# A streaming-encoder step on one core: low sums over four PSUM banks, a root multiplied on GpSimd, activations a step sooner

## The chip, the cores and the metric

The kernel runs on one core of a Trainium2 chip. A core has five engines with queues of their own: TensorE (PE; its weight loads are listed as PEld), VectorE (DVE), ScalarE (ACT), GpSimd (POOL) and SyncE (SP), which here only issues DMAs. The metric is the device time of one execution in microseconds (us).

## The reference, cut to what matters

One layer of an encoder is computed for two request groups that share the weights: 256 frames of a new stream and 64 of a running one. The kernel treats them as T = 320 columns beside each other. All data is float32 with D = 2048 features. The part around the change is the feed-forward half, with D_FF = 5632:

```python
hn = rmsnorm(h, norm_ffn[l])
gu = hn @ w_gate_up[l]
h = h + (jax.nn.silu(gu[..., :D_FF]) * gu[..., D_FF:]) @ w_down[l]
```

Ahead of it come one combined input projection, stick-breaking attention, a spatial gate, two branch projections and an output projection; behind it a last norm.

## The kernel before, in words

Features lie on the 128 partitions, so a weight block is 128 x 128. A float32 product is made of pieces of reduced type: ACT casts a raw weight tile to `wh` (the high part), DVE subtracts to get `wl` (the low part), and activations are split in the same way into a pair. A product then is weight-high times activation-high, plus weight-high times activation-low, plus weight-low times activation-high.

The feed-forward products run in **quads** (`quad`, L542): four output blocks of 128 features at once, 30 quads in all. 22 of them make gates and ups, alternating (a gate quad, then the up quad that belongs to it), 8 of them a part of the down product. A quad has two stages.

- **The main sums** (L565) turn the product round: the activations are the weights of TensorE, and the `wh` of four blocks stream through, 512 columns wide. For each pair of the 16 k-blocks a raw tile of 512 KB is loaded by SP (L549), ACT casts it (L557), DVE subtracts (L558), and ten matmuls follow. 80 matmuls fill three PSUM banks, `main`. Quads alternate between the `acc` banks (three) and the `aux` banks (four).
- **The low sums** (L575): for each of the four blocks b, 16 matmuls of 320 columns with the `wl` as weights, into one bank, which DVE then copies to `total` (L576). The banks were `aux1` (there is one), `aux`, `aux1`, `aux`. So the third block wants the bank that the first has filled, and its first matmul waits until DVE has copied it.

The main sums come out with frames on the partitions and have to be transposed. `quad_turn` takes the upper and the lower 16 bits of each word apart: ACT copies the first plane out of the three banks (L592), DVE the second (L594), and ACT issues one transposing DMA for each (L595). `quad_join` puts the planes together again (L605) and adds them to `total` (L607, L608).

A table of due ticks (`at`, `tick`) sets when this happens; a tick is one weight tile or one low block. Joining is due 10 ticks behind the end of the main sums (6 for the last up quad), so in the middle of the next quad. One and two ticks later the two halves of `total` go on. For a gate (`gate_out`): times `rh`, the reciprocal root of the norm, on DVE (L612), then SiLU on ACT (L613). For an up (`up_out`): times `rh` (L617), times the gate (L618), both on DVE, then a cast on ACT (L621) and subtractions on DVE (L624) that split the result into the pair `act`. So in the quad behind an up quad DVE has more to do than in the quad behind a gate quad.

Buffers near by: three raw tiles, four `wh`, four `wl` and five more low tiles (`low`), two `sum` tiles. Instructions of one engine run in the order in which they stand in its queue.

Of the kernel before, what the change touches and what calls it, by code (L numbers as in the profile page):

```python
# [11 lines left out]
U16 = mybir.dt.uint16  # L12
AF = mybir.ActivationFunctionType
ALU = mybir.AluOpType

P = 128
TP = 256
TS = 64
T = TP + TS
# [15 lines left out]
def stream_step(ctx: ExitStack, tc: tile.TileContext, xT, w_in, w_a, w_b, w_out, w_gu, w_down,  # L35
                gains, ws_t, bs, ck_t, cv, y_t, k_t, v_t, sv_t):
    nc = tc.nc
# [11 lines left out]
    def aux():  # L49
        return psum.tile([P, 512], F32, tag="aux", bufs=4, name="aux")  # L50

    def aux1():
        return psum.tile([P, 512], F32, tag="aux1", bufs=1, name="aux1")
# [4 lines left out]
    def at(tick, fn, *a):  # L58
        assert tick > state["tick"], (tick, state["tick"])
        later.setdefault(tick, []).append((fn, a))  # L60

    def tick():
        state["tick"] += 1
        for fn, a in later.pop(state["tick"], ()):
            fn(*a)

    def halved(raw, n):
        wh = wsplit.tile([P, HALF * P], F32R, tag="wh", name="wh")
        wl = wsplit.tile([P, HALF * P], F32R, tag="wl", name="wl")
        nc.scalar.copy(out=wh[:, : n * P], in_=raw[:, : n * P])  # L70
        state["split"] = nc.vector.tensor_tensor(out=wl[:, : n * P], in0=raw[:, : n * P],  # L71
                                                 in1=wh[:, : n * P].bitcast(F32), op=ALU.subtract)
        return wh, wl

    def weights(src, n):
        state["n"] += 1
        if state["more"] is not None and state["n"] > 3 and state["n"] % 2 == 0:
            raw = state["more"].tile([P, HALF * P], F32, tag="raw2", bufs=3, name="raw2")
        else:
            raw = wraw.tile([P, HALF * P], F32, tag="raw", name="raw")  # L80
        nc.sync.dma_start(out=raw[:, : n * P], in_=src)
        return halved(raw, n)
# [8 lines left out]
    def block(src, act):  # L91
        ps = acc()
        nk = len(act)
        for k0 in range(0, nk, HALF):
            n = min(HALF, nk - k0)
            w = weights(src[:, k0 * P : (k0 + n) * P], n)
            for j in range(n):
                product(ps, w, j, act[k0 + j], k0 + j == 0, k0 + j == nk - 1)
            tick()
        return ps[:, :T]  # L100

    def pair(name, shape=(2, T), dt=F32):
        return big.tile([P, *shape], dt, tag="D", bufs=24, name=name)
# [10 lines left out]
    def t320(tag, bufs=2, dt=F32):  # L114
        return tmp.tile([P, T], dt, tag=tag, bufs=bufs, name=tag)
# [43 lines left out]
    got = {}  # L159
# [36 lines left out]
    with tc.manual_schedule(engines={mybir.EngineType.SP}):  # L196
        load_x(0, 0, 1)
        for i, (b0, nb, c, n) in enumerate(tiles):
# [11 lines left out]
            w = halved(raw, nb * n)  # L210
# [220 lines left out]
    for g in range(H):  # L431
        ps = block(w_in[4 * H + g], xs)
        t = t320("ev")
# [51 lines left out]
    for g in range(H):  # L485
        ps = block(w_in[3 * H + g], xs)
        t = t320("ev")
# [5 lines left out]
    for m in range(KD):  # L493
        gate = []
        for i in range(2):
            ps = block(w_in[5 * H + i * KD + m], xs)
            t = t320("ev")
# [8 lines left out]
        ps = block(w_a[m], aT)  # L506
        t = t320("sq", 1)
        nc.vector.tensor_tensor(out=t, in0=ps, in1=gate[0], op=ALU.mult)
        ps = block(w_b[m], bT)
# [10 lines left out]
    for m in range(KD):  # L520
# [4 lines left out]
        ps = block(w_out[m], merged)  # L525
# [14 lines left out]
    count = [0, 0]  # L540

    def quad(src, xs, done, tag="sum", lag=10):  # L542
        lows = []
        nk = len(xs)
        main = [(acc, aux)[count[1] % 2]() for _ in range(3)]
        count[1] += 1
        for c in range(0, nk, 2):
            raw = wraw.tile([P, HALF * P], F32, tag="raw", name="raw")
            nc.sync.dma_start(out=raw.rearrange("p (b k) -> p b k", b=4),  # L549
                              in_=src[:, :, c * P : (c + 2) * P].rearrange("b p k -> p b k"))  # L550
            wh = wsplit.tile([P, HALF * P], F32R, tag="wh", name="wh")
            if count[0] % 9 < 4:
                wl = wsplit.tile([P, HALF * P], F32R, tag="wl", name="wl")
            else:
                wl = fpool.tile([P, HALF * P], F32R, tag="low", bufs=5, name="low")
            count[0] += 1
            nc.scalar.copy(out=wh, in_=raw)  # L557
            state["split"] = nc.vector.tensor_tensor(out=wl, in0=raw, in1=wh.bitcast(F32), op=ALU.subtract)  # L558
            wh = wh.rearrange("p (b k) -> p b k", b=4)
            lows.append(wl)  # L560
            for j in range(2):
                k = c + j
                w, x = wh[:, :, j * P : (j + 1) * P], xs[k]
                for i, at0 in enumerate((0, T + TS, P, T + TS + P, TP)):
                    nc.tensor.matmul(main[i // 2].rearrange("p (b m) -> p b m", b=4), x[:, at0 : at0 + P], w,  # L565
                                     start=k == 0 and i % 2 == 0, stop=k == nk - 1 and (i % 2 == 1 or i == 4))
            tick()
        total = fpool.tile([P, 4, T], F32, tag=tag, bufs=2 if tag == "sum" else 1, name=tag)
        now = state["tick"]
        turning = quad_turn(main)  # L570
        for b in range(4):
            ps = aux1() if b % 2 == 0 else aux()
            for k in range(nk):
                at0 = (2 * b + k % 2) * P
                nc.tensor.matmul(ps[:, :T], lows[k // 2][:, at0 : at0 + P], xs[k][:, 0:T], start=k == 0, stop=k == nk - 1)  # L575
            copied = nc.vector.tensor_copy(total[:, b, :], ps[:, :T])  # L576
            tick()
        at(now + lag, quad_join, copied.ins, total, *turning)
        for i in range(2):
            at(now + lag + 1 + i, done, total, 2 * i)  # L580
        return total

    def quad_turn(main):
        flat = fpool.tile([P, 12 * P], F32, tag="flat", name="flat")
        turned = fpool.tile([P, 2, 12, P], U16, tag="turned", name="turned")
        planes = flat.bitcast(U16).rearrange("p (i n) -> p i n", i=2)
        for i in range(2):
            for c in range(3):
                hw = main[c].bitcast(U16).rearrange("p (n w) -> p n w", w=2)
                plane = planes[:, i, c * 512 : (c + 1) * 512]  # L590
                if i == 0:
                    tc.keep_in_program_order(nc.scalar.copy(out=plane, in_=hw[:, :, 1 - i]))  # L592
                else:
                    nc.vector.tensor_copy(plane, hw[:, :, 1 - i])  # L594
            nc.scalar.dma_start_transpose(out=turned[:, i], in_=planes[:, i, :])  # L595
        return flat, turned

    def quad_join(behind, total, flat, turned):
        with tc.issue_after(behind), tc.issue_after(state["split"].ins):
            join(total, flat, turned)  # L600
# [9 lines left out]
    def gate_out(total, b):  # L610
        t = total[:, b : b + 2, :]
        nc.vector.tensor_tensor(out=t, in0=t, in1=got["rh"][:, None, :].to_broadcast([P, 2, T]), op=ALU.mult)  # L612
        nc.scalar.activation(out=t, in_=t, func=AF.Silu)  # L613

    def up_out(to, apart, gate, total, b):
        t = total[:, b : b + 2, :]
        nc.vector.tensor_tensor(out=t, in0=t, in1=got["rh"][:, None, :].to_broadcast([P, 2, T]), op=ALU.mult)  # L617
        nc.vector.tensor_tensor(out=t, in0=t, in1=gate[:, b : b + 2, :], op=ALU.mult)  # L618
        for j in range(2):
            a = pair("act", dt=F32R)  # L620
            nc.scalar.copy(out=a[:, 0, :], in_=t[:, j, :])  # L621
            flat = a.rearrange("p i t -> p (i t)")
            for r0, r1, at0 in (((TP, T, T), (0, TP, T + TS)) if apart else ((0, T, T),)):
                nc.vector.tensor_tensor(out=flat[:, at0 : at0 + r1 - r0], in0=t[:, j, r0:r1],  # L624
                                        in1=a[:, 0, r0:r1].bitcast(F32), op=ALU.subtract)
            to.append(a)
# [72 lines left out]
    def gate_quad(b0, tag="sum"):  # L699
        return quad(w_gu[b0 : b0 + 4], wide_x, gate_out, tag)  # L700

    def up_quad(b0, gate, to, apart, lag=10):
        quad(w_gu[KF + b0 : KF + b0 + 4], wide_x, lambda total, b: up_out(to, apart, gate, total, b), lag=lag)
# [15 lines left out]
    for k0, k1 in ((0, HALF), (HALF, n)):  # L719
        for m, ps in enumerate(lead):  # L720
            w = weights(w_down[m][:, (s0 + k0) * P : (s0 + k1) * P], k1 - k0)
# [155 lines left out]
```

## Time and profile before

| what | us |
|---|---|
| median of 3 runs (lowest, highest) | 1694.61 (1692.58, 5915.3) |
| the profiled execution's own time | 1693.54 |
| span of its profile, first to last instruction | 1691.8 |
| TensorE busy in it | 1676.3 |
| VectorE busy | 1063.0 |
| ScalarE busy | 711.8 |
| GpSimd busy | 38.9 |

The highest of the three runs lies far off the other two and is not used. The profile shows one execution. Busy time of matmuls overlaps and says little of how fast they follow each other; that is read from the starts of equal groups of matmuls in the chain of waits or in the timeline, which list each group with its start, its duration and its count. "Idle before" is the time in which an engine waited just ahead of an instruction, with the engine or DMA that released it. ACTq and SPq rows are issues of DMAs.

### The profile page before, as it was taken

The page shows a single profiled execution, that of the slowest core. Times are in us where ns is not written, and L with a number is a line of the kernel's source. Part 1 is how long each engine was busy: PE and PEld are TensorE (multiplying, and loading weights), DVE is VectorE, ACT ScalarE, POOL GpSimd, SP SyncE. Part 2 cuts the span into 40 slices and gives each one's busy share as a digit, 9 for nine tenths or more (in the row PEclk, how much of TensorE's full clock was granted, in tenths as well). Part 3 has the DMA queues.
Part 4 walks back from the last instruction along what each step waited for, and adds up shares of the span by engine and source line. Part 5 has one row for each costly group of instructions (what it writes and reads, how often), then busy time and mean ns, then how long its engine had stood idle before and what let it go on. Part 6 is the DMA issues. An engine that isn't in the chain of part 4 may idle for free.

```text
span 1691.8 us, 25018 instructions
## 1 busy us (share of the span) xinstructions
PE 1676.3 (99%) x10112; PEld 1576.2 (93%) x10112; DVE 1063.0 (63%) x1431; ACT 711.8 (42%) x914; POOL 38.9 (2%) x68
## 2 busy tenths in 40 slices
PE   9999999999999999999999999999999999999998
PEld 9999999999999999998888888988888888888997
DVE  7665656544444445556666766566767666667766
ACT  7555655433333333444443334333434343334343
POOL 1100001000000000000000000000000000000000
PEclk9999999999999999999999999999999999999999
DMA  8766555444444444556566666666666666666554
GB/s 291 245 175 177 160 160 166 116 150 150 150 150 150 151 149 171 173 169 180 162 197 163 188 168 196 172 195 164 192 174 182 175 180 187 179 175 177 166 150 125
DMA packets 286644, 291.75 MB, mean 172 GB/s; under 512 B 123168, under 2 KB 252192, under 8 KB 286528
## 3 DMA queue, kind: packets, MB, share of 16 engines
q1 hardware_dynamic: 188592, 257.72, 47.8%
q10 hardware_dynamic: 95312, 24.17, 8.1%
q0 software_dynamic: 2624, 8.26, 1.5%
q8 instruction: 79, 1.29, 0.3%
q14 instruction: 37, 0.30, 0.1%
HBM read 256.03 MB, written 5.51 MB: 155 GB/s over the span
## 4 chain that ended last, share of the span: by engine, by line
PE 87%; DVE 6%; DMA 5%; issue 2%; ACT 0%; SPq 0%; DVEq 0%; ACTq 0%
PE aux L565 16%; PE acc L87 15%; PE acc L88 15%; PE acc L89 15%; PE aux L575 13%; PE acc L565 8%; DMA raw<-w_gu 4%; DVE low L558 1%; DVE flat L605 1%; DVE act L624 1%; PE aux L89 1%; PE aux L87 1%; PE aux L88 1%; DVE flat L594 1%; PE acc L657 1%
## 5 line engine op out<-in xcount | busy, mean ns | idle before, releaser
L557 ACT CAST wh<-raw 128x1024 fp32r<-128x1024 f32 x240 | 252.7, 1053 | 503.1 <-DMA raw<-w_gu 322.5
L70 ACT CAST wh<-raw 128x1024 fp32r<-128x1024 f32 (+2 forms) x232 | 235.7, 1016 | 412.2 <-PE acc L88 286.4
L71 DVE TENSOR_TENSOR wl<-raw,wh 128x1024 fp32r<-128x1024 f32 (+2 forms) x232 | 274.8, 1187 | 165.6 <-ACT wh L70 165.0
L87 PE MATMUL acc<-A,wh 128*128 128x320 f32 x1088 | 337.8, 311 | 0.2 <-ACT A L108 0.2
L88 PE MATMUL acc<-A,wh 128*128 128x320 f32 x1088 | 336.6, 309 | 0.0
L89 PE MATMUL acc<-A,wl 128*128 128x320 f32 x1088 | 336.3, 309 | 0.0
L87 PEld LDWEIGHTS acc<-A,wh 128*128 128x128 f32 x1088 | 204.5, 188 | 2.2 <-issue 1.5
L88 PEld LDWEIGHTS acc<-A,wh 128*128 128x128 f32 x1088 | 204.6, 188 | 0.2 <-DVE A L110 0.2
L89 PEld LDWEIGHTS acc<-A,wl 128*128 128x128 f32 x1088 | 204.4, 188 | 0.0
L565 PE MATMUL aux<-wh,A 128*128 128x512 f32 x880 | 201.6, 389 | 0.0
L565 PE MATMUL acc<-wh,A 128*128 128x512 f32 x880 | 201.5, 389 | 0.0
L558 DVE TENSOR_TENSOR low<-raw,wh 128x1024 fp32r<-128x1024 f32 x132 | 161.1, 1228 | 58.8 <-ACT wh L557 58.8
L565 PEld LDWEIGHTS aux<-wh,A 128*128 128x128 f32 x880 | 164.7, 188 | 33.7
L565 PEld LDWEIGHTS acc<-wh,A 128*128 128x128 f32 x880 | 164.8, 188 | 33.7
L558 DVE TENSOR_TENSOR wl<-raw,wh 128x1024 fp32r<-128x1024 f32 x108 | 130.9, 1220 | 50.9 <-ACT wh L557 50.9
L575 PE MATMUL aux<-A,low 128*128 128x320 f32 x784 | 131.1, 309 | 2.9 <-DVE sum L576 2.9
L575 PEld LDWEIGHTS aux<-A,low 128*128 128x128 f32 x784 | 119.2, 188 | 4.8 <-DVE sum L576 3.7
L575 PE MATMUL aux<-A,wl 128*128 128x320 f32 x624 | 107.4, 310 | 3.5 <-DVE sum L576 2.8
L576 DVE COPY sum<-aux 128x320 f32<-128x320 f32 x112 | 53.9, 487 | 84.3 <-PE aux L575 84.1
L575 PEld LDWEIGHTS aux<-A,wl 128*128 128x128 f32 x624 | 95.6, 188 | 5.6 <-DVE sum L576 3.9
L87 PE MATMUL acc<-mh,wh 128*128 128x320 f32 x256 | 79.1, 309 | 0.0
L88 PE MATMUL acc<-ml,wh 128*128 128x320 f32 x256 | 79.1, 309 | 0.0
(238 smaller groups left out, 2236.9 us busy)
## 6 DMA issues: line engine op xcount, KB each, us to landing
raw<-w_gu SPq DMA_DIRECT2D x176, 512.0 KB, 4.0
raw<-w_in SPq DMA_DIRECT2D x141, 512.0 KB, 3.7
raw<-w_down SPq DMA_DIRECT2D x80, 512.0 KB, 4.4
raw<-w_out SPq DMA_DIRECT2D x32, 512.0 KB, 3.6
raw<-w_a SPq DMA_DIRECT2D x16, 512.0 KB, 3.5
raw<-w_b SPq DMA_DIRECT2D x16, 512.0 KB, 3.5
raw<-w_down SPq DMA_DIRECT2D x16, 256.0 KB, 2.9
ev<-xT POOLq DMA_DIRECT2D x16, 160.0 KB, 2.6
```

Of the source, the lines that this page charges most:

```text
L70: nc.scalar.copy(out=wh[:, : n * P], in_=raw[:, : n * P])
L71: state["split"] = nc.vector.tensor_tensor(out=wl[:, : n * P], in0=raw[:, : n * P], in1=wh[:, : n * P].bitcast(F32), op=ALU.subtract)
L87: nc.tensor.matmul(ps[:, :T], a, x[0], start=first, stop=False)
L88: nc.tensor.matmul(ps[:, :T], a, x[1], start=False, stop=False)
L89: nc.tensor.matmul(ps[:, :T], b, x[0], start=False, stop=last)
L557: nc.scalar.copy(out=wh, in_=raw)
L558: state["split"] = nc.vector.tensor_tensor(out=wl, in0=raw, in1=wh.bitcast(F32), op=ALU.subtract)
L565: nc.tensor.matmul(main[i // 2].rearrange("p (b m) -> p b m", b=4), x[:, at0 : at0 + P], w, start=k == 0 and i % 2 == 0, stop=k == nk - 1 ...
L575: nc.tensor.matmul(ps[:, :T], lows[k // 2][:, at0 : at0 + P], xs[k][:, 0:T], start=k == 0, stop=k == nk - 1)
L576: copied = nc.vector.tensor_copy(total[:, b, :], ps[:, :T])
L594: nc.vector.tensor_copy(plane, hw[:, :, 1 - i])
L605: nc.vector.tensor_copy(rows[:, :, :, :, 1 - i], turned[:, i].rearrange("p (c b) t -> p b c t", c=3))
```

## The change

Four things change. The first two low blocks of a quad go to two of the banks of the set that this quad's main sums don't use (`others`), the third to `aux1`, the fourth to `aux`. `quad_turn` becomes two functions: `first_plane` stands where `quad_turn` stood, `second_plane` (the three DVE copies and their transposing DMA) is issued behind DVE's copy of the second low block. A gate is multiplied by `rh` once more, after SiLU, by GpSimd, and `up_out` no longer multiplies by `rh`. Both halves of a quad are due one tick behind the joining, where the second half was due two ticks behind.

```diff
     def quad(src, xs, done, tag="sum", lag=10):
         lows = []
         nk = len(xs)
-        main = [(acc, aux)[count[1] % 2]() for _ in range(3)]
+        banks, others = (acc, aux) if count[1] % 2 == 0 else (aux, acc)
+        main = [banks() for _ in range(3)]
         count[1] += 1
...
-        turning = quad_turn(main)
+        turning = first_plane(main)
         for b in range(4):
-            ps = aux1() if b % 2 == 0 else aux()
+            ps = (others, others, aux1, aux)[b]()
             for k in range(nk):
                 at0 = (2 * b + k % 2) * P
                 nc.tensor.matmul(ps[:, :T], lows[k // 2][:, at0 : at0 + P], xs[k][:, 0:T], start=k == 0, stop=k == nk - 1)
             copied = nc.vector.tensor_copy(total[:, b, :], ps[:, :T])
+            if b == 1:
+                with tc.issue_after(copied.ins):
+                    second_plane(main, *turning)
             tick()
         at(now + lag, quad_join, copied.ins, total, *turning)
         for i in range(2):
-            at(now + lag + 1 + i, done, total, 2 * i)
+            at(now + lag + 1, done, total, 2 * i)
         return total
...
+    def half_words(main, c, i):
+        return main[c].bitcast(U16).rearrange("p (n w) -> p n w", w=2)[:, :, 1 - i]
+
+    def first_plane(main):
         flat = fpool.tile([P, 12 * P], F32, tag="flat", name="flat")
         turned = fpool.tile([P, 2, 12, P], U16, tag="turned", name="turned")
+        plane = flat.bitcast(U16)[:, 0 : 12 * P]
+        for c in range(3):
+            tc.keep_in_program_order(nc.scalar.copy(out=plane[:, c * 512 : (c + 1) * 512], in_=half_words(main, c, 0)))
+        nc.scalar.dma_start_transpose(out=turned[:, 0], in_=plane)
         return flat, turned
+
+    def second_plane(main, flat, turned):
+        plane = flat.bitcast(U16)[:, 12 * P : 24 * P]
+        for c in range(3):
+            nc.vector.tensor_copy(plane[:, c * 512 : (c + 1) * 512], half_words(main, c, 1))
+        nc.scalar.dma_start_transpose(out=turned[:, 1], in_=plane)
...
     def gate_out(total, b):
         t = total[:, b : b + 2, :]
         nc.vector.tensor_tensor(out=t, in0=t, in1=got["rh"][:, None, :].to_broadcast([P, 2, T]), op=ALU.mult)
         nc.scalar.activation(out=t, in_=t, func=AF.Silu)
+        nc.gpsimd.tensor_tensor(out=t, in0=t, in1=got["rh"][:, None, :].to_broadcast([P, 2, T]), op=ALU.mult)
 
     def up_out(to, apart, gate, total, b):
         t = total[:, b : b + 2, :]
-        nc.vector.tensor_tensor(out=t, in0=t, in1=got["rh"][:, None, :].to_broadcast([P, 2, T]), op=ALU.mult)
         nc.vector.tensor_tensor(out=t, in0=t, in1=gate[:, b : b + 2, :], op=ALU.mult)
```

The lines move with it: before and after correspond as L557 and L558 (cast), L558 and L559 (subtraction), L575 and L576 (low matmuls), L576 and L577 (their copies), L592 and L595 (first plane), L594 and L602 (second plane), L595 and L596 with L603 (transposes), L605 and L612 (joining), L612 and L619, L618 and L625, L621 and L628 (cast of `act`), L624 and L631. GpSimd's multiplication is L621 of the changed kernel.

Three places show how the instructions stand. The first is TensorE in the sixth quad, an up quad whose main sums lie in `aux`: the low matmuls, of which the numbered names are tiles of `aux1`. Before:

```order
L575 MATMUL aux_8973<-A,low 128x320 x10
L575 MATMUL aux_8973<-A,wl 128x320 x6
L575 MATMUL aux<-A,low 128x320 x10
L575 MATMUL aux<-A,wl 128x320 x6
L575 MATMUL aux_9009<-A,low 128x320 x10
L575 MATMUL aux_9009<-A,wl 128x320 x6
```

and after:

```order
L576 MATMUL acc<-A,low 128x320 x10
L576 MATMUL acc<-A,wl 128x320 x6
L576 MATMUL acc<-A,low 128x320 x10
L576 MATMUL acc<-A,wl 128x320 x6
L576 MATMUL aux_9011<-A,low 128x320 x10
L576 MATMUL aux_9011<-A,wl 128x320 x6
```

The first two blocks now go to the idle `acc` banks, and only the third to `aux1`.

The second place is VectorE in the quad behind an up quad (the 27th, main sums in `acc`), where the activations are made and the low sums copied. Before:

```order
L617 TENSOR_TENSOR sum<-sum,rh 128x640 x2
L618 TENSOR_TENSOR sum<-sum,held 128x640 x2
L624 TENSOR_TENSOR act<-sum,act 128x320 x4
L594 COPY flat<-acc 128x512 x3
L576 COPY sum<-aux_13727 128x320
L576 COPY sum<-aux 128x320
L576 COPY sum<-aux_13763 128x320
L558 TENSOR_TENSOR wl<-raw,wh 128x1024 x2
```

and after:

```order
L625 TENSOR_TENSOR sum<-sum,held 128x640 x2
L631 TENSOR_TENSOR act<-sum,act 128x320 x4
L577 COPY sum<-aux 128x320 x2
L602 COPY flat<-acc 128x512 x3
L577 COPY sum<-aux_13763 128x320
L559 TENSOR_TENSOR wl<-raw,wh 128x1024 x2
```

The two multiplications by `rh` are gone, and the copies of the first two low blocks stand ahead of the second plane's copies; the two subtractions keep their place behind the third block's copy.

The third place is ScalarE in the same quad. Before:

```order
L557 CAST wh<-raw 128x1024 x7
L621 CAST act<-sum 128x320 x4
L592 COPY flat<-acc 128x512 x3
L557 CAST wh<-raw 128x1024
L595 DMA_TRANSPOSE turned<-flat 128x12x128 x2
L557 CAST wh<-raw 128x1024 x6
```

and after:

```order
L558 CAST wh<-raw 128x1024 x6
L628 CAST act<-sum 128x320 x4
L558 CAST wh<-raw 128x1024
L595 COPY flat<-acc 128x512 x3
L558 CAST wh<-raw 128x1024
L596 DMA_TRANSPOSE turned<-flat 128x12x128
L603 DMA_TRANSPOSE turned<-flat 128x12x128
L558 CAST wh<-raw 128x1024 x6
```

The casts of `act` stand one weight cast earlier. The second transpose stands where it stood, ahead of the casts for the rest of the next quad's weights, though what it waits for is now made later.

More of the change, by code (lines that the diff above doesn't have):

```diff
@@ L579, in quad @@
         for i in range(2):
-            at(now + lag + 1 + i, done, total, 2 * i)
+            at(now + lag + 1, done, total, 2 * i)
         return total
-    def quad_turn(main):
+    def half_words(main, c, i):
+        return main[c].bitcast(U16).rearrange("p (n w) -> p n w", w=2)[:, :, 1 - i]
+    def first_plane(main):
         flat = fpool.tile([P, 12 * P], F32, tag="flat", name="flat")
         turned = fpool.tile([P, 2, 12, P], U16, tag="turned", name="turned")
[L586 to L595, printed above, removed]
-        return flat, turned
+        plane = flat.bitcast(U16)[:, 0 : 12 * P]
+        for c in range(3):
+            tc.keep_in_program_order(nc.scalar.copy(out=plane[:, c * 512 : (c + 1) * 512], in_=half_words(main, c, 0)))
+        nc.scalar.dma_start_transpose(out=turned[:, 0], in_=plane)
+        return flat, turned
+    def second_plane(main, flat, turned):
[3 more added lines that the diff above has]
+        nc.scalar.dma_start_transpose(out=turned[:, 1], in_=plane)
     def quad_join(behind, total, flat, turned):
```

## The prediction

> **What bounds the kernel now.** I read the page's first part, then TensorE's waits, then the chain of waits, which lists the long groups of matmuls by their starts.
>
> ```profile
> span 1691.8 us, 25018 instructions
> PE 1676.3 (99%) x10112; PEld 1576.2 (93%) x10112; DVE 1063.0 (63%) x1431; ACT 711.8 (42%) x914; POOL 38.9 (2%) x68
> PE aux L575 <- DVE sum L576: 5.7, 7, 1.1
> PE aux L575 <- DVE held L576: 0.7, 1, 0.7
> ```
>
> TensorE is busy all the time; VectorE and ScalarE have room. Among TensorE's few waits the only one that comes back is that of a low matmul (L575) for VectorE's copy of an earlier low sum (L576). Ends of matmuls are modelled, so 6.4 us is not yet its price. Starts in the chain of waits are safer (start, length, what):
>
> ```profile
> 788.50 18.16 PE aux L565 x80
> ...
> 1040.87 18.16 PE acc L565 x80
> ...
> 1095.95 18.16 PE acc L565 x80
> ...
> 1513.30 18.16 PE aux L565 x80
> ```
>
> The rows at 1040.87 and 1095.95 are two quads of the down product apart, in which nothing waits: 55.08 us, so a quad costs 27.54 when TensorE runs freely. From 788.50 (the second quad) to 1513.30 (the 28th) lie 26 quads, which free would take 26 x 27.54 = 716.04. They took 724.80. So **8.76 us** are gaps, some 0.8 to 1.3 us behind most up quads. The last three quads have none:
>
> ```profile
> 1513.13 3.14 PE L565 MATMUL aux<-wh,A 128*128 128x512 f32 x13
> 1595.76 0.31 PE L87 MATMUL acc<-act,wh 128*128 128x320 f32 x1
> ```
>
> 1595.76 - 1513.13 = 82.63, three times 27.54. The timeline shows how a gap comes about, here in the ninth quad, which has the activations of an up quad to make:
>
> ```profile
> 1000.46 1.55 DVE L617 TENSOR_TENSOR sum<-sum,rh 128x640 f32<-128x640 f32 x2
> 1001.93 1.55 DVE L618 TENSOR_TENSOR sum<-sum 128x640 f32<-128x640 f32 x2
> 1002.87 1.04 PE L575 MATMUL aux<-A,wl 128*128 128x320 f32 x6
> 1003.66 1.54 ACT L621 CAST act<-sum 128x320 fp32r<-128x320 f32 x4
> 1004.15 1.97 DVE L624 TENSOR_TENSOR act<-sum,act 128x64 fp32r<-128x64 f32 x8 [0.68 <-ACT act L621]
> 1006.04 1.88 DVE L594 COPY flat<-acc 128x512 uint16<-128x512 uint16 x3
> 1007.84 0.88 DVE L576 COPY held<-aux 128x320 f32<-128x320 f32 x2
> 1008.37 1.14 PE L575 MATMUL aux<-A,wl 128*128 128x320 f32 x6 [0.65 <-DVE held L576]
> 1011.43 2.35 DVE L558 TENSOR_TENSOR wl<-raw,wh 128x1024 fp32r<-128x1024 f32 x2
> 1013.17 18.32 PE L565 MATMUL aux<-wh,act 128*128 128x512 f32 x80
> ```
>
> The low sums start at 1002.87 and should be over 9.38 later, at 1012.25; the next main sums start at 1013.17. The first block is finished about 1005.2, but VectorE is in L624 and L594 until 1007.84, the copy ends at 1008.3, and the third block, which wants the same bank, begins at 1008.37 instead of 1007.5: 0.92 us.
>
> **The change part by part.**
>
> *Banks.* The third low block takes the one `aux1` bank, last read a whole quad (27.5 us) before. The first two take banks of the idle set: their last readers were the plane copies of the quad before, done ahead of its own last low block. Looking one quad on: the next main sums need these two banks as their second and third, and the copies are done by 1008.3 in the quad above, against 1013.17. No low matmul then waits for VectorE. Gain: the whole 8.76 us, if nothing new comes up.
>
> *Second plane.* It is the quad behind a gate quad that shows best what the shift moves, since there nothing is late:
>
> ```profile
> 973.46 1.47 ACT L613 ACTIVATE sum<-sum 128x640 f32<-128x640 f32 x2
> 977.53 3.31 ACTq L595 DMA_TRANSPOSE turned<-flat  x2
> 980.22 0.49 DVE L576 COPY sum<-aux 128x320 f32<-128x320 f32 x1 [1.37 <-PE aux L575]
> 982.57 0.49 DVE L576 COPY sum<-aux 128x320 f32<-128x320 f32 x1 [1.86 <-PE aux L575]
> 982.97 2.35 DVE L558 TENSOR_TENSOR wl<-raw,wh 128x1024 fp32r<-128x1024 f32 x2
> 984.71 18.32 PE L565 MATMUL acc<-wh,A 128*128 128x512 f32 x80
> 988.06 1.05 ACT L557 CAST wh<-raw 128x1024 fp32r<-128x1024 f32 x1 [9.51 <-DMA raw<-w_gu]
> 991.23 1.05 ACT L557 CAST wh<-raw 128x1024 fp32r<-128x1024 f32 x1 [2.13 <-DMA raw<-w_gu]
> 993.46 1.98 DVE L605 COPY flat<-turned 128x1536 uint16<-128x1536 uint16 x2
> ```
>
> The three copies take 1.88 (row L594 above). Behind the second block's copy they run from 980.7 to 982.6, just ahead of the third block's copy at 982.57, so the subtractions at 982.97, which free the raw tiles for the next loads, move by about 0.1 us. The second transpose is issued at 982.6 instead of about 979.2, and ScalarE's queue waits for it.
>
> ```profile
> L595 ACTq DMA_TRANSPOSE turned<-flat x60: 1438/1658/2663, 780.1 to 1590.3; - x60
> DMA to landing us min/median/max: 3.7/4.0/5.8
> ```
>
> An issue holds the queue 1.66 us, until 984.3. Behind it stand the weight casts, and the first of those waits for its raw tile until 988.06: 3.8 us of cover, cost 0. The plane lands at 986.6, at worst 988.4, and the joining (L605) reads it at 993.46: again covered. Without cover each would cost its own lateness in every quad. In the last up quad, whose joining is due four ticks earlier, this leaves next to nothing, but its low weights are needed only some us later.
>
> What can suffer is the weights, because the transpose now shares the DMA engines with the first loads behind the low sums (stretch, PE, PEld, DVE, ACT, POOL busy, clock, DMA share, GB/s):
>
> ```profile
> 981.00:985.00 4.00, 4.00 (x29) 3.96 (x28) 2.44 (x3) 0.00 (x0) 0.00 (x0) 1.00 1.01 85
> 985.00:989.00 4.00, 4.00 (x19) 3.32 (x18) 1.86 (x3) 0.94 (x1) 0.00 (x0) 1.00 0.79 248
> 993.00:997.00 4.00, 4.00 (x20) 3.30 (x19) 4.00 (x5) 1.74 (x2) 0.00 (x0) 1.00 0.45 149
> ```
>
> While transposes run, the DMA engines are full and move only 85 GB/s; in the new place that stretch falls on loads that already take a share of 0.79. How long may these be late? Four `wh` are in hand when the main sums start; a tick takes 18.16 / 8 = 2.27. The fifth is needed at 984.71 + 9.08 = 993.8 and cast by 989.1 (4.7 to spare), the sixth at 996.1 and cast by 992.3 (**3.8 to spare**). The cost is bounded below by nothing and above by the whole median landing of 4.0 put in front of the loads: 0.2 per quad, 6 us over 30. I take 0, since the share of 0.45 a few us later lets the loads catch up, and keep 6 for the range.
>
> *The multiplication on GpSimd.* VectorE loses 22 instructions:
>
> ```profile
> L617 DVE TENSOR_TENSOR sum<-sum,rh 128x640 f32<-128x640 f32 x22 | 17.1, 815 | 0.0
> ```
>
> That is 1.57 us in each quad behind an up quad, in front of the very copies that are late. With the banks spread this buys nothing more on TensorE. GpSimd gets 22, a kind of instruction that this trace does not have there. The nearest rows:
>
> ```profile
> L237 POOL TENSOR_SCALAR_AFFINE_SELECT mask<-mask 128x128 f32<-128x128 f32 x3 | 1.8, 630 | 0.0
> L137 POOL PARTITION_ALL_REDUCE whole<-sq_h x1 | 2.1, 2147 | 16.1 <-DVE sq_h L156 16.1
> ```
>
> From below VectorE's own 0.8 us; from above the reduction, 2.15 for 320 columns, so 4.3 for 640. Five selects of 128 columns, 3.2, lie nearest in kind; I take 3. The two follow SiLU from 974.2 on and are done by 980.2, at the upper bound by 982.8. Their reader is the gate's multiplication (L618) in the next quad, at 1001.93 for the gates of 973.46. So this costs nothing.
>
> *Activations a step sooner.* The four casts of `act` (1.54) go ahead of one weight cast and start about 2.3 us sooner, since VectorE is done with L618 by 1002. The weight cast behind them (one for the third or fourth tick of the next quad, 10 us away) may move by 0.4 us. Cost 0; VectorE's wait of 0.68 before L624 shrinks, off the path.
>
> **Sum.** 1693.54 (the profiled execution; 1.7 of it lies outside the span) - 8.76 = 1684.8. The median of the runs is 1.07 higher, which would give 1685.9. I forecast the middle, 1685.3, that is 0.5% less.
>
> **The rivals.**
>
> *The wait moves (0.09).* Releasers are inferred, and a gap could stay for a wait that the copy hides, such as the subtraction of the next `wl`. For it: VectorE stays the busiest helper in these quads. Against: each gap is followed by free running, and in the down quads with the same weights none exists. With half of the gaps left, 1693.5 - 4.4 = 1689; with all, 1694.
>
> *Slower, by the weights (0.06).* The second transpose delays the loads by more than the 3.8 us to spare, and TensorE waits for the sixth `wh` of every quad. It makes up for the gain from 3.8 + 8.76 / 30 = 4.1 us. At the longest landing, 5.8, it costs 2.0 x 30 = 60, and the time is 1685 + 60 = 1745. For it: the full DMA engines at 981 to 985. Against: the transposes' share is brief, and the loads behind have room.
>
> *Slower, by GpSimd against VectorE (0.02).* If the two multiplications last beyond 982.97, 4.4 us each, VectorE's subtractions, which read two tensors, may have to wait for them, and raw tiles come free late. With 3.8 us to spare it decides from 6.3 us each; at 8.6, twice the upper bound, the second ends at 991.4, 8.4 late, so 4.6 x 11 = 51 us: 1736. The rows above show GpSimd with nearly nothing to do, so they don't tell what the two do to each other. The Trainium skill ("SBUF — State Buffer", Who interferes with whom) says that a VectorE instruction with two inputs in SBUF and a GpSimd instruction that reads SBUF exclude each other for their whole length; its "GPSIMD Engine Reference" (Performance versus the Vector engine) measures 2.6 cycles of 1.2 GHz per element, by which 640 columns would be 1.4 us as an estimate. By that rule with that figure the two would be done at 977.0, before such an instruction starts, and the sum would stay as it is; no run here shows either yet.
>
> **How the numbers follow.** Forecast 0.83, the rivals 0.09, 0.06 and 0.02. The lower end is the lowest run less the gain, 1692.58 - 8.76 = 1683.8, and half the distance between the two near runs (1692.58 and 1694.61) below that: 1682.8. The upper end takes in a delay of 6 us by the weights (1691.3) and the wait that moves in full: 1694. A measurement of this kernel tells about 2% (34 us) from no change. Faster by that would need more than all the idle time of TensorE in the span (15.5): 0.01. Slower by that are the outer parts of the two slower rivals: 0.03. Within: 0.96.
>
> **What the changed profile would show.** Right: no wait of L576 for a copy L577; quads behind up quads 27.54 apart like the rest; second transposes issued some 7 us behind the main sums' end; GpSimd's multiplications over before the subtractions. Wrong: main matmuls (L566) waiting for `wh` or for a bank, subtractions stretched beside GpSimd's instructions, or gaps that stay.

## The result and the profile after

The changed kernel takes 1684.84 us in the median of five runs (1684.77 to 1685.37), against 1692.58 in the median of five for the kernel before beside it (four of the five lie between 1692.21 and 1694.61, the fifth, at 5915.3, far off); the ratio is 0.9954, with a 95% interval of 0.9939 to 0.9968. The profiled span falls from 1691.8 to 1683.0 us. The runs also lie closer together: 0.6 us from lowest to highest, where eleven runs of the kernel before, taken beside the experiments, went from 1689.76 to 1697.14.

The page of the changed kernel, its span, busy times and the engines of the chain that ended last:

```profile
span 1683.0 us, 25074 instructions
PE 1673.5 (99%) x10112; PEld 1575.6 (94%) x10112; DVE 1048.0 (62%) x1409; ACT 712.4 (42%) x914; POOL 73.2 (4%) x90
PE 99%; DMA 0%; DVE 0%; SPq 0%; ACT 0%; issue 0%; DVEq 0%
```

The same last row of the kernel before:

```profile
PE 87%; DVE 6%; DMA 5%; issue 2%; ACT 0%; SPq 0%; DVEq 0%; ACTq 0%
```

So the chain used to leave TensorE, for VectorE, DMAs and issues, for 13% of the span; now it stays there. TensorE's waits in the profile are these three, none of them in a quad:

```profile
PE aux L165 <- POOL eps_t L124: 1.0, 1, 1.0
PE acc L87 <- ACT A L108: 0.6, 1, 0.6
PE acc L752 <- ACT sq L646: 0.5, 1, 0.5
```

The starts of the main sums in the chain, first, second and last quad:

```profile
760.99 18.16 PE acc L566 x80
788.53 18.16 PE aux L566 x80
...
1559.65 18.16 PE aux L566 x80
```

From 760.99 to 1559.65 are 29 quads in 798.66 us, exactly 29 x 27.54: no quad has a gap left. The timeline of the ninth quad, which had a gap of 0.92 us before:

```profile
995.66 1.55 DVE L625 TENSOR_TENSOR sum<-sum 128x640 f32<-128x640 f32 x2
997.30 1.53 ACT L628 CAST act<-sum 128x320 fp32r<-128x320 f32 x4
997.78 1.98 DVE L631 TENSOR_TENSOR act<-sum,act 128x64 fp32r<-128x64 f32 x8 [0.56 <-ACT act L628]
999.30 1.04 PE L576 MATMUL aux<-A,wl 128*128 128x320 f32 x6
1001.85 0.49 DVE L577 COPY held<-aux 128x320 f32<-128x320 f32 x1 [2.09 <-PE aux L576]
1004.60 1.88 DVE L602 COPY flat<-acc 128x512 uint16<-128x512 uint16 x3
1006.54 0.49 DVE L577 COPY held<-aux 128x320 f32<-128x320 f32 x1
1006.95 2.35 DVE L559 TENSOR_TENSOR wl<-raw,wh 128x1024 fp32r<-128x1024 f32 x2
1008.68 7.67 PE L566 MATMUL aux<-wh,act 128*128 128x512 f32 x33
```

VectorE is done with the activations at 999.8 and then waits 2.09 us for the first low block, where before the block waited for VectorE. From 999.30 to 1008.68 are 9.38 us, the bare low sums. The quad behind a gate quad, with GpSimd's two multiplications, the second transpose and the next weight casts:

```profile
970.75 3.11 POOL L621 TENSOR_TENSOR sum<-sum,rh 128x640 f32<-128x640 f32 x2 [51.88 <-ACT sum L620]
978.97 1.43 ACTq L603 DMA_TRANSPOSE turned<-flat  x1
979.41 2.35 DVE L559 TENSOR_TENSOR wl<-raw,wh 128x1024 fp32r<-128x1024 f32 x2
981.14 18.32 PE L566 MATMUL acc<-wh,A 128*128 128x512 f32 x80
984.69 1.05 ACT L558 CAST wh<-raw 128x1024 fp32r<-128x1024 f32 x1 [9.73 <-DMA raw<-w_gu]
986.41 1.05 ACT L558 CAST wh<-raw 128x1024 fp32r<-128x1024 f32 x1 [0.66 <-DMA raw<-w_gu]
```

The fifth cast starts 3.55 us behind the main sums' start (3.35 before), the sixth 5.27 (6.52 before). This quad isn't typical: its sixth cast was the latest of all quads before. Over all quads but the first, the median of the fifth cast goes from 3.29 to 3.60 and that of the sixth from 5.81 to 6.00, so both come a little later; the latest fifth cast now starts 5.15 behind, where it may start 8.03 behind (9.08 less its own 1.05).

### The profile page after: what moved, and what is told of

Its sections match the earlier page's. It is cut to its first block, busy times and chain, and to the rows that moved or that the text cites. A ratio compares the mean times of both kernels' runs of the same rounds, so it can differ in the third digit from the quotient of the medians.

```text
span 1683.0 us, 25074 instructions
## 1 busy us (share of the span) xinstructions
PE 1673.5 (99%) x10112; PEld 1575.6 (94%) x10112; DVE 1048.0 (62%) x1409; ACT 712.4 (42%) x914; POOL 73.2 (4%) x90
## 4 chain that ended last, share of the span: by engine, by line
PE 99%; DMA 0%; DVE 0%; SPq 0%; ACT 0%; issue 0%; DVEq 0%
PE aux L566 16%; PE acc L566 16%; PE acc L87 15%; PE acc L88 15%; PE acc L89 15%; PE aux L576 13%; PE acc L576 4%; PE aux L89 1%; PE aux L88 1%; PE aux L87 1%; PE acc L664 1%; PE acc L680 1%; PE aux L664 1%; DMA x<-xT 0%; PE aux L462 0%; PE aux L365 0%
## 5 line engine op out<-in xcount | busy, mean ns | idle before, releaser
L558 ACT CAST wh<-raw 128x1024 fp32r<-128x1024 f32 x240 | 252.6, 1053 | 494.5 <-DMA raw<-w_gu 331.2
L559 DVE TENSOR_TENSOR low<-raw,wh 128x1024 fp32r<-128x1024 f32 x132 | 161.5, 1231 | 60.6 <-ACT wh L558 60.5
L559 DVE TENSOR_TENSOR wl<-raw,wh 128x1024 fp32r<-128x1024 f32 x108 | 131.1, 1221 | 54.3 <-ACT wh L558 54.3
L576 PE MATMUL aux<-A,low 128*128 128x320 f32 x588 | 98.1, 309 | 0.0
L576 PEld LDWEIGHTS aux<-A,low 128*128 128x128 f32 x588 | 89.4, 188 | 0.4
L576 PE MATMUL aux<-A,wl 128*128 128x320 f32 x468 | 80.2, 309 | 0.0
L89 PE MATMUL acc<-mh,wl 128*128 128x320 f32 x256 | 79.2, 309 | 0.0
L577 DVE COPY sum<-aux 128x320 f32<-128x320 f32 x82 | 40.1, 489 | 61.1 <-PE aux L576 59.4
```

What stands on the lines that cost most here:

```text
L89: nc.tensor.matmul(ps[:, :T], b, x[0], start=False, stop=last)
```

## The experiments

The theory is that the gaps were one wait, that of the third low block for the copy of the first, and that whatever ends this wait brings the whole gain. Its rivals are that the banks alone can do it, or that the lateness moves on to the weights.

**The banks alone**, on the kernel before:

```diff
-            ps = aux1() if b % 2 == 0 else aux()
+            ps = (others, others, aux1, aux)[b]()
```

> The kernel before with the banks alone (first two low blocks in the idle main set, third in aux1, fourth in aux). Theory: the gaps are only the third low block's wait for the copy of the first, so the banks alone take all of it: span 1683.0 as with the whole change, against 1691.8 before, no wait of a low matmul for a copy. Rival (VectorE's late work is what costs, and it moves on): a part of the 8.8 us stays, span 1685 to 1690, with TensorE waiting for a bank or for weights elsewhere.

Measured: 1684.79 us (1684.71 to 1684.93), ratio 0.9950 (0.9934 to 0.9967), span 1682.9. No low matmul waits. The banks bring everything that the whole change brings.

**The second plane alone**, with the banks as before:

```diff
-        turning = quad_turn(main)
+        turning = first_plane(main)
...
             copied = nc.vector.tensor_copy(total[:, b, :], ps[:, :T])
+            if b == 1:
+                with tc.issue_after(copied.ins):
+                    second_plane(main, *turning)
```

> The kernel before with the second plane alone behind the copy of the second low block; the banks are aux1, aux, aux1, aux as before. By the timeline of before, in the ninth quad the subtractions for act end at 1006.1, so the copy of the first low block would end at 1006.6, ahead of the third block's natural start at 1007.5. Theory (a wait for this copy and nothing else): the gaps close here too, span 1683 to 1684. Rival (only a free bank closes them): half or more of the 8.8 us stays, span 1687 or more.

Measured: 1685.32 us (1684.75 to 1686.58), ratio 0.9954 (0.9939 to 0.9969), span 1684.8. The profile is of the slowest of the five runs, and its span is above the 1683 to 1684 expected, but not by the quads: the first and the last start at 760.76 and 1559.70, so all gaps together are 0.3 us, and 1.5 us are one wait behind them, of the last products (L663) for `h`. In the ninth quad (first copy, then the third block's first matmuls):

```profile
999.87 1.97 DVE L630 TENSOR_TENSOR act<-sum,act 128x64 fp32r<-128x64 f32 x8 [0.58 <-ACT act L627]
1001.76 0.48 DVE L576 COPY held<-aux 128x320 f32<-128x320 f32 x1
...
1003.77 1.04 PE L575 MATMUL aux<-A,wl 128*128 128x320 f32 x6
```

The copy is over at 1002.24, 1.5 us ahead of the block that wants the bank. So the order of VectorE's copies is enough too.

**The multiplication on GpSimd alone**, with banks and second plane as before:

```diff
         nc.scalar.activation(out=t, in_=t, func=AF.Silu)
+        nc.gpsimd.tensor_tensor(out=t, in0=t, in1=got["rh"][:, None, :].to_broadcast([P, 2, T]), op=ALU.mult)
...
-        nc.vector.tensor_tensor(out=t, in0=t, in1=got["rh"][:, None, :].to_broadcast([P, 2, T]), op=ALU.mult)
         nc.vector.tensor_tensor(out=t, in0=t, in1=gate[:, b : b + 2, :], op=ALU.mult)
```

> The kernel before with the multiplication by the root moved to GpSimd alone; banks and second plane as before. VectorE has 1.57 us less to do ahead of the late copies, and the casts of act stand one weight cast sooner. In the ninth quad the copies would then end at about 1007.0, half a us ahead of the third block at 1007.5. Theory: nearly all gaps close, span 1683 to 1685, with 0.5 us to spare. Rival (VectorE only waits longer for ScalarE): the gaps stay, span 1689 to 1692.

Measured: 1685.09 us (1684.85 to 1685.78), ratio 0.9952 (0.9937 to 0.9967), span 1683.8. The gaps are gone here as well, but for 0.7 us over all quads (its first and last quad start at 761.05 and 1560.41, so 799.36 for 29). The casts of `act` stand one weight cast earlier in this kernel too, though its due ticks are those of before.

**All but the banks:**

```diff
-            ps = (others, others, aux1, aux)[b]()
+            ps = aux1() if b % 2 == 0 else aux()
```

> The whole change with the banks undone (aux1, aux, aux1, aux again). Theory: the first block's copy stands ahead of the second plane and VectorE is done early, so the copy ends about 2.8 us behind the main sums and the third block, 4.7 behind them, never waits: span 1683.0. Rival (the banks carry the gain): the gaps come back, span 1690 or more.

Measured: 1685.11 us (1684.58 to 1686.71), ratio 0.9953 (0.9937 to 0.9968), span 1683.3. The banks aren't needed when VectorE is early.

The fourth edit, activations a step sooner, has no run of its own: put alone into the kernel before it builds into the same order of instructions on every engine, and taken out of the changed kernel it leaves that order as it is. (Only the numbers in the tiles' names differ.)

**VectorE made late, without and with the banks.** Three extra multiplications per half, with unused results:

```diff
             to.append(a)
+        for _ in range(3):
+            nc.vector.tensor_tensor(out=spare, in0=t[:, 0, :], in1=t[:, 1, :], op=ALU.mult)
```

> The kernel before with six extra VectorE multiplications of 320 columns (about 0.45 us each, results unused) behind each up quad's activations, so the copies of the low sums come about 2.5 us later there. Theory: each of 11 gaps grows by about 2 us, span 1691.8 + 22 = 1714 (1708 to 1720), all of it as a wait of the third low block for the first one's copy. Rival (the extra work is hidden like other VectorE work): below 1697.

> The same extra VectorE work, on the kernel before with the banks alone. Theory: with the third block in its own bank TensorE no longer waits for copies, so the lateness costs nothing: span 1683 to 1684. Rival (the lateness goes on to the weights, since the subtractions that free raw tiles stand behind the copies): span above 1690, with main matmuls waiting for wh.

Measured, one run each: without the banks 1702.50 us, beside 1694.89 for the kernel before; span 1700.7. With the banks 1684.70, span 1682.9. TensorE's waits without the banks, and, in the ninth quad, the matmuls ahead of the wait, the two copies and the block that waited:

```profile
PE aux L576 <- DVE sum L577: 12.6, 8, 2.9
PE aux L576 <- DVE held L577: 2.8, 2, 1.5
```

```profile
1009.92 0.90 PE L576 MATMUL aux<-A,wl 128*128 128x320 f32 x5
1011.54 0.88 DVE L577 COPY held<-aux 128x320 f32<-128x320 f32 x2
1012.08 1.14 PE L576 MATMUL aux<-A,wl 128*128 128x320 f32 x6 [1.27 <-DVE held L577]
```

and the same copies with the banks:

```profile
1005.51 1.40 DVE L578 COPY held<-aux 128x320 f32<-128x320 f32 x3
1006.82 2.35 DVE L560 TENSOR_TENSOR wl<-raw,wh 128x1024 fp32r<-128x1024 f32 x2
```

The kind of wait is the one expected, its size is not: the gaps grow to 18.0 us (760.48 to 1577.13 for the same 29 quads, less 798.66), not to some 31. The six extra instructions are 0.48 us each, 2.9 in all, but two of them run while VectorE waited for ScalarE's casts anyway, so that the first copy comes only 1.3 us later against the main sums' end (6.3 instead of 5.0 behind it). And the order of TensorE's instructions is another one in this kernel: in ten quads four or five matmuls of the fourth block stand ahead of the third block, as in the row at 1009.92. A low matmul takes 9.38 / 64 = 0.147 us, so five of them fill 0.73 us of the wait. In the ninth quad the third block starts 1.35 us later than before against the main sums' end, but the gap grows by only 0.6.

With the banks three copies run late in a row at 1005.51, and no matmul waits. This room is what the banks add. How much of it the other two edits have wasn't run under the same load; in the ninth quad their first copies are over 1.5 us (second plane) and 1.7 us (GpSimd) before the bank is wanted.

**More transposing**, on the changed kernel: the first plane's transpose issued once more, and in a second kernel the second plane's as well.

```diff
         nc.scalar.dma_start_transpose(out=turned[:, 1], in_=plane)
+        nc.scalar.dma_start_transpose(out=turned[:, 0], in_=flat.bitcast(U16)[:, 0 : 12 * P])
+        nc.scalar.dma_start_transpose(out=turned[:, 1], in_=plane)
```

> The whole change with the first plane's transposing DMA issued once more behind the second's in every quad (the same data to the same place), so that the loads behind the low sums meet twice the transposing. Theory (the weights have 3.8 us or more to spare): casts of the fifth and sixth weight tile 1 to 2 us later, span 1683 to 1684. Rival (the weights stand at the edge): TensorE waits for wh in each quad, 1 us x 30, span 1710 or more.

> As the run before with the second plane's transpose issued once more too; its issue waits for the landing of the one before, about 3.8 us, and holds ScalarE's queue until about the time of the fifth cast. Theory: loads up to 4 us later, which the 3.8 to 5 us to spare just hold or just don't: span 1683 to 1700. Rival (no cover): 2 us or more in every quad, span 1743 or more.

Measured, one run each: 1717.81 us with one more, 1844.37 with two, beside 1694.89 for the kernel before. My expectation failed in both. With one more, the added issue (L604) stands in the built order ahead of the second plane's (L603), not behind it as was meant. TensorE's first waits, then the issues of L603, then the ninth quad and the tenth:

```profile
PE aux L566 <- ACT wh L558: 8.1, 11, 2.2
PE acc L566 <- ACT wh L558: 7.3, 10, 1.2
```

```profile
L603 ACTq DMA_TRANSPOSE turned<-flat x30: 1815/4729/6230, 787.2 to 1616.9; - x30
```

```profile
981.35 2.08 ACTq L604 DMA_TRANSPOSE turned<-flat  x1
983.48 4.73 ACTq L603 DMA_TRANSPOSE turned<-flat  x1
988.30 1.05 ACT L558 CAST wh<-raw 128x1024 fp32r<-128x1024 f32 x1 [9.71 <-PE acc L566]
...
1013.80 3.64 ACTq L603 DMA_TRANSPOSE turned<-flat  x1
1017.54 2.95 ACT L558 CAST wh<-raw 128x1024 fp32r<-128x1024 f32 x3 [9.53 <-issue]
1018.63 6.66 PE L566 MATMUL aux<-wh,act 128*128 128x512 f32 x28 [0.53 <-ACT wh L558]
```

An issue that takes ScalarE's queue 1.45 us in the changed kernel now takes 4.73 in the median, and the fifth cast starts at 988.30 as soon as the queue is free, 6.99 behind the main sums' start at 981.31 instead of 3.55. It is over at 989.35, still ahead of 990.39 (981.31 + 9.08), when TensorE wants it, so the ninth quad loses nothing, nor do those ahead of it. In the tenth, whose main sums start at 1008.85, the fifth cast starts only 8.69 behind and TensorE waits. From there to the last main sums, at 1584.41, 20 quads take 575.56 us instead of 550.80: 24.8 of the 33.0 us by which the span is longer. Another 4.9 are one wait just behind the quads. So the cover of some 4 us is real, but it is cover of ScalarE's queue as much as of the loads, and one transpose more per quad uses it up. Whether the long issue comes from the DMA engines' load or from something in the queue itself, these runs don't tell.

**GpSimd reading in the middle of VectorE's work**, on the changed kernel:

```diff
             lows.append(wl)
+            for i in range(2):
+                nc.gpsimd.tensor_tensor(out=spare, in0=wl[:, 0:T].bitcast(F32), in1=wl[:, T : 2 * T].bitcast(F32), op=ALU.mult)
```

> The whole change with two more GpSimd multiplications of 320 columns per weight tile of a quad, from the low weights into an unused tile, so that GpSimd reads in the middle of VectorE's subtractions. Theory (nothing of the change overlaps, so it could not show): VectorE's subtraction takes longer than its 1.23 us wherever the two meet, up to 0.8 us more, but TensorE stays free, span 1683 to 1690. Rival (the engines don't disturb each other): subtraction 1.23, span 1683.

Measured, one run: 1752.19 us, beside 1692.03 for the kernel before. The subtractions of this kernel (one of their two rows), its joining copies, the range of the added instructions (minimum, median, maximum in ns), a stretch in which both engines are busy, and three of TensorE's waits (L569 main sums, L579 low sums, L580 copies of the low sums):

```profile
L560 DVE TENSOR_TENSOR low<-raw,wh 128x1024 fp32r<-128x1024 f32 x132 | 208.8, 1592 | 56.3 <-ACT wh L559 55.5 <-POOL sq L564 0.8
L615 DVE COPY flat<-turned 128x1536 uint16<-128x1536 uint16 x60 | 99.7, 1715 | 4.3 <-DMA turned<-flat 4.3
```

```profile
L564 POOL TENSOR_TENSOR sq<-low x264: 857/1551/2018, 789.4 to 1644.7; 128x320 f32<-128x320 f32 x132
```

```profile
1012.21 13.57 POOL L564 TENSOR_TENSOR sq<-low 128x320 f32<-128x320 f32 x8 [1.23 <-DVE low L560]
1016.42 1.88 DVE L560 TENSOR_TENSOR low<-raw,wh 128x1024 fp32r<-128x1024 f32 x1
1018.23 2.16 DVE L617 TENSOR_TENSOR sum<-flat,sum 128x1280 f32<-128x1280 f32 x1
```

```profile
PE acc L569 <- ACT wh L559: 11.3, 8, 2.9
PE acc L579 <- DVE low L560: 6.9, 6, 1.7
PE aux L569 <- DVE sum L580: 5.8, 7, 2.6
```

A subtraction takes 1.59 us instead of 1.23, a joining copy 1.72 instead of 1.05, and GpSimd's 320 columns 1.55 instead of 0.86 at best. The direction was expected; that TensorE would stay free was not. It waits for weights and for low parts, and now and then the next main sums wait for the copy of a low sum, whose bank they want: a VectorE that is late enough holds up TensorE with the new banks too. So what the rival "slower, by GpSimd against VectorE" rests on does happen where the two engines meet. The changed kernel escapes it by the place of its multiplications: in the quad shown above they are over by 973.9, and VectorE's next instruction with two inputs starts at 979.41. Nor do the other 20 multiplications meet one; all 22 took between 1.57 and 1.59 us.

## Why the prediction was right

*The gaps.* 8.76 us were forecast to go, and 8.8 went from the span; the quads follow each other at 27.54, as in the down product before. The steps that counted on nothing else holding TensorE were right for this kernel. What the sum really forecast is the time without gaps, since the gaps were taken from the same execution as the span. The gain itself depends on the execution it is counted from: the spans of the eleven runs before go from 1688.0 to 1695.4 us, so it is 5 to 12 us. That their gaps differ would explain it, but only one of the kernel before is profiled. Nine of its quads lost time, 0.25 to 1.34 us each. That the measured 1684.84 lies at the lower of the two sums that were averaged agrees with this: the 1.07 by which a median of before lay above the profiled execution had no counterpart in the changed kernel. And the measurement can tell much smaller differences from no change than the 2% that the prediction gave it: the interval of the ratio is 0.3% wide.

*The banks.* That they suffice is shown by the run with them alone. The prediction said that, with them, the other edits buy nothing on TensorE; that holds. It did not see that either the order of the copies or the relief of VectorE suffices alone. The rows quoted there already said so: the first copy was 0.9 us late, and each of these two edits takes more than 1.5 us from in front of it. (The second copy there ends at 1008.7, not by 1008.3 as the prediction has it for both; against 1013.17 that changes nothing.)

*The second plane.* Subtractions that keep their place and an issue that ScalarE's queue can bear: both as forecast (the issue 7.2 us behind the main sums, 1.45 long, landing after 3.8 in the median). The weights came a little later, 0.3 us for the fifth cast and 0.2 for the sixth in the median, far inside what they had to spare; with the banks alone, where the second plane keeps its place, the fifth stays at 3.29. The quad that the prediction went by, with its sixth cast at 991.23, was the latest of all in this. In the last up quad the joining did wait 2.6 us for the second plane, as feared, and TensorE didn't. The upper bound of 6 us was reasoned from the landing alone; the runs with more transposes show that the queue's own time, which grows when transposes crowd, has to be in it.

*GpSimd.* I took 3 us for a multiplication from the row of the selects; it is 1.58, and since it was covered either way the sum did not suffer. The figure of the Trainium skill ("GPSIMD Engine Reference", Performance versus the Vector engine), by which the estimate was 1.4 us, lay nearer. The rule of the Trainium skill in "SBUF — State Buffer" (Who interferes with whom), that a VectorE instruction with two SBUF inputs and a GpSimd instruction that reads SBUF exclude each other, agrees with the last run in that both get longer (1.59 instead of 1.23, 1.55 instead of 0.86); there they go one for one, each stretched: from one subtraction to VectorE's next instruction are 1.81 us (1016.42 to 1018.23), in which one added instruction has its turn too, and alone the two last 1.23 and 0.86, 2.09 together. So it is close to a taking of turns, but not for the whole length: some 0.3 us of the two still overlap.

*Activations a step sooner.* Here the working was wrong. The earlier casts of `act` were put down to this edit; they come from the removal of VectorE's multiplication, for the order built from the step alone is that of before, and the kernel with GpSimd alone has them. As the step was forecast to cost and gain nothing, the sum did not suffer.

## What to carry to other kernels

Measure a gap by the starts of equal groups of work, and ask how late the late thing is before asking how to remove its cause: 0.9 us of lateness can be undone by an order, by a lighter engine or by a buffer, and only one of them is needed. Of these the buffer held when the other engine was made later still, until that engine was loaded so much that the next stage wanted the same bank. It also went with a steadier time: the five runs lie within 0.6 and 0.2 us in the two kernels with the banks, within 0.9 to 2.1 in the three without. Of an edit to due times, look first whether the built order changes at all.

## What was not expected of the hardware

The time that a transposing DMA's issue holds ScalarE's queue is no constant: in the median 1.45 us for each of the changed kernel's two per quad, 1.66 for the two back to back before, 4.73 for the last of three. And GpSimd's reading slows VectorE's joining copies of 16-bit planes, which have one input (1.05 to 1.72 us), even more than its subtractions with two (1.23 to 1.59). Copies out of PSUM banks are not slowed: in the same run those of the low sums that lie wholly beside a GpSimd instruction take 0.48 us like the others, those of the second plane 0.68. In the kernel with two more transposes, where TensorE waited for casts for 98 us, the mean granted clock was 0.964 instead of 0.998; no run here separates the waiting from the clock.
